# The channel mixer's residual of layer 1, prepared per token tile beside feature tiles 4 to 7

## The chip, the cores and the metric

One NeuronCore of a Trainium2 chip runs the whole program. The time is that of one execution on the device in microseconds (us). TensorE (PE, with its weight loads as PEld), VectorE (DVE), ScalarE (ACT) and GpSimd (POOL) each work through a queue of their own in order and wait for each other by semaphores; SyncE (SP) issues nearly all DMAs, also in order.

## The reference

A decoder trunk of two layers over 1024 tokens of width 1024. Layer 1 (`l == 0` in the code) has an RWKV-7 mixer, layer 2 (`l == 1`) a sparse attention; each is followed by a dense channel mixer. What matters here:

```
x   = layernorm(ALPHA * x + (1 + gt1) * mixer(hin), ln_g[i, 0], ln_b[i, 0])
hin = x * (1 + sc2) + sh2
y   = (silu(hin @ w_gate) * (hin @ w_up)) @ w_out          # 1024 -> 2816 -> 1024
x   = layernorm(ALPHA * x + (1 + gt2) * y, ln_g[i, 1], ln_b[i, 1])
```

shift, scale and gate come from a projection of the conditioning vector by `ada_w`, whose parts for later sub-layers the kernel computes while the channel mixer of layer 1 runs.

## The kernel before

Everything is float32. A matrix product is made of three passes: each operand is split into a rounded part `hi` and a rest `lo`, and hi*hi, hi*lo and lo*hi are added in PSUM. For weights, ACT casts a loaded tile (`wst`, 3 buffers) to `whi`, and `wlo` is the difference, formed on DVE twice and on POOL once in every three (list `low`).

The channel mixer is `ffn`. Tokens go in two halves (`hf`) of 512, each four token tiles of 128. The 2816 hidden features are 22 feature tiles of 128, in three groups (`FG`: 0 to 7, 8 to 14, 15 to 21). For each feature tile `j` of a group `gate_up` makes 24 + 24 matmuls into the two banks `psu`: the gate, which ACT evacuates by silu, and the up product, which DVE multiplies onto it (tile `sl`, L1167) and splits into `hid`. The gate of tile j+1 may overwrite the gate's bank as soon as silu is done; the up product of tile j+1 needs the other bank, and so L1167 of tile j. After a group, the hidden tiles are multiplied by rows of `w_out` (banks `psg` and `psx`), and `evac_y` adds the result times the gate vector `G` onto the residual tiles `R`.

The residual (`resid`, L799 and L800) takes the normalised, not yet scaled rows of the sub-layer before and applies gain and bias in place: two POOL operations on 128x1024 for each token tile. `ln_tiles` loads the gate vector `G` (from DRAM, where `ada_done` put it), and the gain and bias rows of the layer norm, spread over 128 partitions, into two tiles of the pool `z4` (8 buffers of 128x1024, function `big`), and multiplies both by ALPHA on DVE (L783, L784). In the first half the rows are there already (`zt`, tiles `R` that the input preparation also reads); in the second each is loaded from DRAM (L798) into a buffer `R` (4) once the first half has written its own.

In the text, all of this stands once per half behind the loop over feature tiles 0 to 7. In the same loop stand pieces of the `ada_w` projection (`ada_v`, L300 to L311): four loads of 128x1024 into `z4` tiles and eight DVE operations on 128x512 (L305, L307) each. They stand at feature tiles 4, 6 and every second one from 8 in the first half, and at 0, 2, 4, 6, 8 in the second. The pool `z4` opens only when the tail of the RWKV mixer is through, beside feature tile 3 of the first half.

A planner sets the order on each engine: it walks through a modelled time and gives an engine, whenever it is free, the instruction that stands first in the text among those whose operands and buffers are ready. So an instruction can be placed well before others that stand ahead of it in the text. The order is fixed then; on the chip an engine waits at an instruction until its semaphores say it can start.

Of the kernel before, what the change touches and what calls it, by code (L numbers as in the profile page):

```python
# [24 lines left out]
NTT = HN // P  # L25
# [51 lines left out]
def dap(ap, off, dims):  # L77
    return bass.AP(tensor=ap.tensor, offset=ap.offset + off, ap=[list(d) for d in dims])
# [3 lines left out]
def trunk(ctx, tc, a, out):  # L82
# [3 lines left out]
    def pool(st, name, bufs=1, space=None, side=None):  # L86
        kw = {} if space is None else {"space": space}
        if side:
            kw["side"] = side
        return st.enter_context(tc.tile_pool(name=name, bufs=bufs, reuse_waits="tile", **kw))  # L90
# [23 lines left out]
    def act(o, i, f=AF.Identity, **kw):  # L114
        return A.activation(o, i, f, **kw)  # L115
# [8 lines left out]
    def hilo(hi, lo, x, eng=G):  # L124
        V.tensor_scalar(hi, x, 1.0, None, op0=OP.mult)
        sub(eng, lo, x, hi)
# [112 lines left out]
    def proj_fm(w, off, ld, xhi, xlo, ncol=P, c=slice(0, 512)):  # L239

        wh, wl = wcols(w, off, ld, ncol)
        o = psx(bank[0])
        for k in range(KT):
            mm3(o[:ncol, c], wh[k], wl[k], xhi[k][:, c], xlo[k][:, c], k == 0, k == KT - 1)
        return o
# [525 lines left out]


    gbp = pool(ctx, "gb", side="right")
    def ln_tiles(l, s, big):
        g = gbp.tile([P, D], F32, tag="G", name="G")
        dma(g, dap(modd[l], (24 * s + 16) * P, [[0, P], [1, D]]))
        if 2 * l + s == 0:
            return g, None, None
        i = 2 * l + s - 1
        lg, lb = big(), big()  # L780
        dma(lg, dap(a["ln_g"], i * D, [[0, P], [1, D]]))
        dma(lb, dap(a["ln_b"], i * D, [[0, P], [1, D]]))
        V.tensor_scalar(lg, lg, ALPHA, None, op0=OP.mult)  # L783
        V.tensor_scalar(lb, lb, ALPHA, None, op0=OP.mult)  # L784
        return g, lg, lb

    def resid(l, s, hf, tt, lnt, r=None):

        held = r is not None
        if not held:  # L790
            r = p2.tile([P, D], F32, tag="R", bufs=2, name="R") if l + s == 0 else rtile()
        i = 2 * l + s
        if i == 0:
            dma(r, a["x"][0, hf * HN + tt * P:hf * HN + tt * P + P, :])
            V.tensor_scalar(r, r, ALPHA, None, op0=OP.mult)
        else:
            if not held:
                dma(r, zd[i - 1][hf][tt * P:tt * P + P, :])  # L798
            G.tensor_tensor(r, r, lnt[1], op=OP.mult)  # L799
            G.tensor_tensor(r, r, lnt[2], op=OP.add)  # L800
        return r
# [57 lines left out]
    def big():  # L859
        return bp[0].tile([P, D], F32, tag="z4", bufs=8, name="z4")  # L860
# [3 lines left out]
    def rtile():  # L864
        return rz.tile([P, D], F32, tag="R", bufs=4, name="R")
# [41 lines left out]
    if True:  # L907
# [181 lines left out]
        lnt = {}  # L1089
# [14 lines left out]
        for gc in range(17):  # L1104
            hf, c = gc // 8, gc % 8
# [13 lines left out]
            if gc == 14:  # L1119
                zt = [rtile() for _ in range(NTT)]  # L1120
# [34 lines left out]
    def ffn(l, hfs, zt, step=lambda gate: None, x=None, pairs=False):  # L1155
        with ExitStack() as st:
            tp = pool(st, f"ffn{l}{hfs[0]}")
            yt = lambda: tp.tile([P, 512], F32, tag="yt", bufs=2, name="yt")
            win, wo = a["ffn_w_in"], a["ffn_w_out"]
            bi, bo_ = l * D * 2 * FH, l * FH * D  # L1160

            def gate_up(j, c, h_, l_):
                og = proj_fm(win, bi + j * P, 2 * FH, *x, c=c)
                sl = tp.tile([P, HN], F32, tag="sl", bufs=2, name="sl")
                act(sl[:, c], og[:, c], AF.Silu)
                ou = proj_fm(win, bi + FH + j * P, 2 * FH, *x, c=c)
                V.tensor_tensor(sl[:, c], sl[:, c], ou[:, c], op=OP.mult)  # L1167
                hilo(h_[:, c], l_[:, c], sl[:, c], V)

            for hf in hfs:  # L1170
                for g, (j0, j1) in enumerate(FG):
                    hh, hl = [], []
                    hid = lambda: tp.tile([P, HN], F32R, tag="hid", bufs=16, name="hid")
                    if g == 0 and pairs:
                        for q in range(2):
                            if q:
                                hin_pair(2 * l + 1, q, zt, *x)
                            for j in range(NPAIR):
                                if q == 0:
                                    hh.append(hid())  # L1180
                                    hl.append(hid())
                                gate_up(j, slice(q * 256, q * 256 + 256), hh[j], hl[j])
                                step(hl[j])
                    after = lastg[0]
                    for j in range(j0 + len(hh), j1):
                        hh.append(hid())
                        hl.append(hid())
                        gate_up(j, slice(0, HN), hh[-1], hl[-1])
                        step(hl[-1])
                        if l == 0 and hf == 0 and j in (4, 6):  # L1190
                            ada_v(0, 8 + j // 2, big, yt)
                            if j == 6:
                                ada_done(0, yt, 40, 48)
                        if l == 0 and hf == 0 and j >= 8 and j % 2 == 0:
                            ada_v(1, j // 2 - 4, big, yt)
                        if l == 0 and hf == 1 and j < 10 and j % 2 == 0:
                            ada_v(1, 7 + j // 2, big, yt)
                        if l == 0 and hf == 1 and j == 10:
                            ada_done(1, yt)
                            hin_vec(1, 0)  # L1200
                            hin_vec(1, 1)
                            bt.append(bias_table(hf32))
                        if l == 0 and hf == 1 and j >= 10:
                            take(bt[0], 1)
                    if g == 0:
                        lnt = ln_tiles(l, 1, big)
                        with tc.issue_after(after.ins) if pairs else ExitStack():
                            rr = [resid(l, 1, hf, tt, lnt, zt[tt] if hf == hfs[0] else None) for tt in range(NTT)]
                    if g == 2 and hf != hfs[-1]:
                        x = hin_prep(2 * l + 1, hf + 1)  # L1210
                    for tt2, n in ([(None, 0), (None, 1)] if g < 2 or l == 0 else [(0, 0), (0, 1), (1, 0), (1, 1)]):
                        tts = range(NTT) if tt2 is None else range(2 * tt2, 2 * tt2 + 2)
                        o = quad() if tt2 is None else [psg(), psx("gx"[n])]
                        for k2 in range(0, j1 - j0, 2):
                            nk = min(2, j1 - j0 - k2)
                            wh, wl = wrows(wo, j0 + k2, nk, bo_ + n * 512, D)
                            step(wl[0])
                            for i_, tt in enumerate(tts):
                                for i in range(nk):
                                    k = k2 + i  # L1220
                                    mm3(o[i_], hh[k][:, tt * P:tt * P + P], hl[k][:, tt * P:tt * P + P],
                                        wh[i], wl[i], k == 0, k == j1 - j0 - 1)
                        for i_, tt in enumerate(tts):
                            evac_y(rr[tt], o[i_], n, lnt, yt)
                        if tt2 is not None and n == 1:
                            if l == 1 and tt2 == 0:
                                fin.clear()
                                for nm in ("ln_g", "ln_b"):
                                    fin.append(big())
                                    dma(fin[-1], dap(a[nm], 3 * D, [[0, P], [1, D]]))  # L1230
                            for tt in tts:
                                if l == 1 and hf == 0 and tt2 == 1:
                                    pend.append((l, 1, hf, tt, rr[tt]))
                                else:
                                    layernorm(l, 1, hf, tt, rr[tt], tp)
                if l == 0:
                    for tt in range(NTT):
                        layernorm(l, 1, hf, tt, rr[tt], tp)
# [9 lines left out]
    with kw:  # L1248
# [346 lines left out]
        zt, x = attention(0)  # L1595
# [4 lines left out]
        zt, x = attention(1)  # L1600
# [28 lines left out]
```

## Time and profile before

| | us |
|---|---|
| median of 3 runs | 3300.29 (3296.58 to 3302.11) |
| the profiled execution | 3298.0 |
| its span from first to last instruction | 3296.2 |
| PE busy | 3057.3 (93%) |
| DVE busy | 2171.1 (66%) |
| POOL busy | 993.3 (30%) |
| channel mixer of layer 1 | about 990 to 1800 of the span |

Times in the rows below count from the start of the span. Busy time on PE is that of pipelined matmuls: two that follow each other at full rate start 0.23 us apart although each lasts 0.39 us.

### The profile page before, as it was taken

Reading aid. Unit: us, or ns where it says so; the run is one execution under the profiler, and the core shown is the slowest. Engines: PE = TensorE matmul, PEld = TensorE weight load, DVE = VectorE, ACT = ScalarE, POOL = GpSimd, SP = SyncE. Lnnn points to the kernel's source line nnn. Section 1 sums busy time; section 2 is a strip of 40 time slices with the busy share of each in tenths; the row PEclk is TensorE's granted clock in tenths of the full one; section 3 lists DMA queues with packets and bytes.
Section 4 is the critical chain, followed back from the end, with each engine's and each line's share of the span. In section 5 each row is a group of like instructions: output and inputs, shape, how many; then the busy total and the mean of one; then the engine's idle time right before and its main releaser. Section 6 shows DMA issues by size and latency. Waiting matters only on the chain. (4 is left out here: it accounts for less than half of the span.)

```text
span 3296.2 us, 48948 instructions
## 1 busy us (share of the span) xinstructions
PE 3057.3 (93%) x17857; PEld 2416.9 (73%) x17857; DVE 2171.1 (66%) x4255; ACT 1350.1 (41%) x2510; POOL 993.3 (30%) x780
## 2 busy tenths in 40 slices
PE   7887999889999999999899999988999999899998
PEld 2465467677877788888688776677887777687886
DVE  4676988647776765494245487886697788775345
ACT  3552463234444222332223655647522566452223
POOL 3351254101113411241113213555222432443111
PEclk8988989979999999999999999998999999999999
DMA  6465465788864665382534432154333421253333
GB/s 196 135 190 152 105 193 142 150 157 178 177 153 121 214 198 161 117 272 90 122 97 127 144 90 68 60 156 122 97 95 105 138 63 34 92 168 100 93 99 122
DMA packets 603460, 436.33 MB, mean 132 GB/s; under 512 B 200338, under 2 KB 500882, under 8 KB 603218
## 3 DMA queue, kind: packets, MB, share of 16 engines
q1 hardware_dynamic: 603218, 433.19, 46.7%
q8 instruction: 141, 2.31, 0.3%
q14 instruction: 101, 0.83, 0.1%
HBM read 378.07 MB, written 54.90 MB: 131 GB/s over the span
## 5 line engine op out<-in xcount | busy, mean ns | idle before, releaser
L204 ACT CAST whi<-wst 128x512 fp32r<-128x512 f32 x886 | 540.5, 619 | 1229.8 <-PE psu L234 533.5
L121 POOL TENSOR_TENSOR wlo<-wst,whi 128x512 fp32r<-128x512 f32 x330 | 459.0, 1391 | 1514.6 <-ACT whi L204 1472.7
L121 DVE TENSOR_TENSOR wlo<-wst,whi 128x512 fp32r<-128x512 f32 (+1 forms) x556 | 474.4, 857 | 509.1 <-ACT whi L204 504.0
L233 PE MATMUL psu<-hin,whi 128*128 128x512 f32 (+1 forms) x1568 | 584.7, 373 | 45.6 <-DVE sl L1167 29.2
L234 PE MATMUL psu<-hin,whi 128*128 128x512 f32 (+1 forms) x1568 | 584.4, 373 | 9.8 <-DVE hin L900 3.3
L235 PE MATMUL psu<-hin,wlo 128*128 128x512 f32 (+1 forms) x1568 | 582.2, 371 | 0.1
L233 PEld LDWEIGHTS psu<-hin,whi 128*128 128x128 f32 x1568 | 299.5, 191 | 101.1 <-DVE sl L1167 32.6
L234 PEld LDWEIGHTS psu<-hin,whi 128*128 128x128 f32 x1568 | 300.2, 191 | 60.6 <-DVE hin L900 3.5
L235 PEld LDWEIGHTS psu<-hin,wlo 128*128 128x128 f32 x1568 | 300.3, 192 | 50.4 <-POOL wlo L121 0.6
L234 PE MATMUL psg<-wlo,hid 128*128 128x512 f32 x528 | 206.3, 391 | 0.0
L233 PE MATMUL psg<-whi,hid 128*128 128x512 f32 x528 | 205.1, 391 | 0.0
L235 PE MATMUL psg<-whi,hid 128*128 128x512 f32 x528 | 205.0, 389 | 0.0
L233 PE MATMUL psg<-xs,whi 128*128 128x512 f32 x384 | 163.2, 434 | 19.4 <-ACT whi L204 10.7
L234 PE MATMUL psg<-xs,whi 128*128 128x512 f32 x384 | 162.9, 425 | 13.2 <-POOL xs L121 10.6
L235 PE MATMUL psg<-xs,wlo 128*128 128x512 f32 x384 | 161.9, 422 | 3.0 <-DVE wlo L121 3.0
L1167 DVE TENSOR_TENSOR sl<-sl,psu 128x512 f32<-128x512 f32 (+1 forms) x98 | 61.7, 630 | 140.2 <-PE psu L235 131.0
L233 PEld LDWEIGHTS psg<-xs,whi 128*128 128x128 f32 x384 | 77.0, 201 | 53.4 <-ACT whi L204 13.5
L233 PEld LDWEIGHTS psg<-whi,hid 128*128 128x128 f32 x528 | 99.1, 188 | 21.0
L235 PEld LDWEIGHTS psg<-whi,hid 128*128 128x128 f32 x528 | 99.1, 188 | 20.8
L234 PEld LDWEIGHTS psg<-wlo,hid 128*128 128x128 f32 x528 | 99.2, 188 | 20.6 <-DVE wlo L121 0.4
L115 ACT ACTIVATE z<-z,mx 128x128 f32<-128x128 f32 (+7 forms) x128 | 99.2, 776 | 33.0 <-DVE mx L1532 32.0
L234 PEld LDWEIGHTS psg<-xs,whi 128*128 128x128 f32 x384 | 76.9, 200 | 42.2 <-POOL xs L121 14.5
(417 smaller groups left out, 6500.7 us busy)
## 6 DMA issues: line engine op xcount, KB each, us to landing
wst<-in_ffn_w_in_dram SPq DMA_DIRECT2D x196, 512.0 KB
wst<-in_ffn_w_out_dram SPq DMA_DIRECT2D x92, 512.0 KB
z<-in_ada_w_dram SPq DMA_DIRECT2D x56, 512.0 KB
wst<-in_rwkv_w_rkv_dram SPq DMA_DIRECT2D x48, 512.0 KB
wst<-in_rwkv_w_out_dram SPq DMA_DIRECT2D x64, 256.0 KB
wst<-in_dsa_w_out_dram SPq DMA_DIRECT2D x32, 512.0 KB
wst<-in_dsa_w_in_dram SPq DMA_DIRECT2D x26, 512.0 KB
wst<-in_ada_w_dram SPq DMA_DIRECT2D x24, 512.0 KB
```

The lines of the kernel that those rows point to most:

```text
L115: return A.activation(o, i, f, **kw)
L121: i = eng.tensor_tensor(lo, x, hi.bitcast(F32), op=OP.subtract)
L204: A.copy(h_[:, :m], st[:, c:c + m])
L233: mm(o, lh, rh, start=first, stop=False)
L234: mm(o, lh, rl, start=False, stop=False)
L235: mm(o, ll, rh, start=False, stop=last)
L1167: V.tensor_tensor(sl[:, c], sl[:, c], ou[:, c], op=OP.mult)
```

## The change

`ln_tiles` is cut in two: the part that loads and scales gain and bias becomes `ln_aff`, and `ln_tiles` takes its result when there is one. In layer 1, in both halves, `ln_aff` now stands in the loop right behind feature tile 4, ahead of that tile's `ada_v`; and `resid` of token tile 0 to 3 stands behind feature tile 4, 5, 6 and 7. The gate vector `G` is loaded where it was. Layer 2 keeps its order.

```diff
-    def ln_tiles(l, s, big):
+    def ln_tiles(l, s, big, aff=None):
         g = gbp.tile([P, D], F32, tag="G", name="G")
         dma(g, dap(modd[l], (24 * s + 16) * P, [[0, P], [1, D]]))
         if 2 * l + s == 0:
             return g, None, None
+        return (g,) + (aff or ln_aff(l, s, big))
+
+    def ln_aff(l, s, big):
         i = 2 * l + s - 1
         lg, lb = big(), big()
         dma(lg, dap(a["ln_g"], i * D, [[0, P], [1, D]]))
         dma(lb, dap(a["ln_b"], i * D, [[0, P], [1, D]]))
         V.tensor_scalar(lg, lg, ALPHA, None, op0=OP.mult)
         V.tensor_scalar(lb, lb, ALPHA, None, op0=OP.mult)
-        return g, lg, lb
+        return lg, lb
...
                     after = lastg[0]
+                    if g == 0:
+                        rr = []
                     for j in range(j0 + len(hh), j1):
                         hh.append(hid())
                         hl.append(hid())
                         gate_up(j, slice(0, HN), hh[-1], hl[-1])
                         step(hl[-1])
+                        if l == 0 and g == 0 and j >= 4:
+                            if j == 4:
+                                aff = ln_aff(l, 1, big)
+                            rr.append(resid(l, 1, hf, j - 4, (None,) + aff, zt[j - 4] if hf == hfs[0] else None))
                         if l == 0 and hf == 0 and j in (4, 6):
                             ada_v(0, 8 + j // 2, big, yt)
...
                     if g == 0:
-                        lnt = ln_tiles(l, 1, big)
+                        lnt = ln_tiles(l, 1, big, aff if rr else None)
                         with tc.issue_after(after.ins) if pairs else ExitStack():
-                            rr = [resid(l, 1, hf, tt, lnt, zt[tt] if hf == hfs[0] else None) for tt in range(NTT)]
+                            rr = rr or [resid(l, 1, hf, tt, lnt, zt[tt] if hf == hfs[0] else None) for tt in range(NTT)]
```

## Rows read from the trace of the kernel before

**Rows 1.** The page, part 1: busy us (share of the span) xinstructions.
```profile
PE 3057.3 (93%) x17857; PEld 2416.9 (73%) x17857; DVE 2171.1 (66%) x4255; ACT 1350.1 (41%) x2510; POOL 993.3 (30%) x780
```

**Rows 2.** Windows: length, busy us (x) of PE, PEld, DVE, ACT, POOL; clock, DMA.
```profile
1076.35:1091.73 15.38, 15.38 (x74) 12.82 (x73) 14.99 (x22) 4.10 (x7) 2.58 (x3) 1.00 1.06 366
1091.73:1115.40 23.67, 19.19 (x82) 15.47 (x81) 23.60 (x12) 4.22 (x7) 23.67 (x10) 0.93 0.58 191
...
1120.00:1200.00 80.00, 80.00 (x358) 66.36 (x358) 49.15 (x70) 19.55 (x32) 12.70 (x9) 1.00 0.61 189
...
1400.00:1440.00 40.00, 40.00 (x186) 33.36 (x184) 36.21 (x66) 15.25 (x22) 10.84 (x9) 1.00 0.81 270
1440.00:1480.00 40.00, 39.34 (x178) 32.30 (x178) 39.67 (x38) 9.27 (x16) 29.53 (x13) 1.00 0.86 279
```

**Rows 3.** Timeline of PE around its stall: start, length, instruction [idle before <- releaser].
```profile
1099.19 0.39 PE L235 MATMUL psu<-hin,wlo 128*128 128x512 f32 x1
1104.06 0.66 PE L233 MATMUL psu<-hin,whi 128*128 128x512 f32 x1 [4.48 <-DVE sl L1167]
...
1107.80 0.39 PE L233 MATMUL psu<-hin,whi 128*128 128x512 f32 x1
```

**Rows 4.** Timeline of POOL in the first half.
```profile
1085.58 1.29 POOL L121 TENSOR_TENSOR wlo<-wst,whi 128x512 fp32r<-128x512 f32 x1 [6.80 <-ACT whi L204]
1091.73 11.13 POOL L799 TENSOR_TENSOR R<-R,z 128x1024 f32<-128x1024 f32 x4 [4.86 <-DVE z L783]
1102.82 2.80 POOL L800 TENSOR_TENSOR R<-R,z 128x1024 f32<-128x1024 f32 x1
1105.58 1.46 POOL L121 TENSOR_TENSOR wlo<-wst,whi 128x512 fp32r<-128x512 f32 x1
1107.00 8.43 POOL L800 TENSOR_TENSOR R<-R,z 128x1024 f32<-128x1024 f32 x3
```

**Rows 5.** Timeline of DVE in the same stretch.
```profile
1076.35 0.49 DVE L305 TENSOR_SCALAR yt<-z,csr 128x512 f32<-128x512 f32 x1 [1.00 <-DMA z<-in_ada_w_dram]
1076.87 4.82 DVE L307 SCALAR_TENSOR_TENSOR yt<-z,csr,yt 128x512 f32<-128x512 f32 x5
...
1083.65 0.68 DVE L1167 TENSOR_TENSOR sl<-sl,psu 128x512 f32<-128x512 f32 x1
...
1090.96 0.69 DVE L783 TENSOR_SCALAR z<-z 128x1024 f32<-128x1024 f32 x1
...
1092.16 2.89 DVE L307 SCALAR_TENSOR_TENSOR yt<-z,csr,yt 128x512 f32<-128x512 f32 x1
1094.98 2.89 DVE L784 TENSOR_SCALAR z<-z 128x1024 f32<-128x1024 f32 x1
...
1100.58 2.82 DVE L121 TENSOR_TENSOR wlo<-wst,whi 128x512 fp32r<-128x512 f32 x1
1103.33 0.67 DVE L1167 TENSOR_TENSOR sl<-sl,psu 128x512 f32<-128x512 f32 x1
```

**Rows 6.** Timeline of SP's issues in the first half.
```profile
1070.07 5.25 SPq L300 DMA_DIRECT2D z<-in_ada_w_dram  x4
...
1075.88 3.70 SPq L300 DMA_DIRECT2D z<-in_ada_w_dram  x4
1079.67 0.65 SPq L781 DMA_DIRECT2D z<-in_ln_g_dram  x1
```

**Rows 7.** Timeline of SP's issues in the second half.
```profile
1416.83 1.10 SPq L300 DMA_DIRECT2D z<-in_ada_w_dram  x2
...
1429.08 0.53 SPq L798 DMA_DIRECT2D R<-z  x1
...
1440.21 3.26 SPq L781 DMA_DIRECT2D z<-in_ln_g_dram  x1
...
1444.00 0.90 SPq L798 DMA_DIRECT2D R<-z  x2
```

**Rows 8.** Timeline of PE at its stall in the second half.
```profile
1457.32 0.50 PE L233 MATMUL psu<-hin,whi 128*128 128x512 f32 x1 [0.66 <-DVE sl L1167]
```

## The prediction

> **What bounds the kernel now.** The first view to read is the busy time of the engines. PE is busy for 93% of the span and DVE for 66% [rows 1]: what makes the kernel longer or shorter is what makes PE wait. The second is a table of windows through the channel mixer of layer 1. Where only weights and hidden tiles are worked on, PE has no idle time and runs at full clock (80.00 of 80.00 us in 1120 to 1200). In the two stretches with the residual it loses time: 19.19 busy of 23.67 us at a granted clock of 0.93 in the first half, 39.34 of 40.00 in the second. In both DVE is busy throughout (23.60 of 23.67 and 39.67 of 40.00) [rows 2].
>
> The third view is the timeline of each engine through 1076 to 1115. PE stops at 1099.4 and starts again at 1104.06, an idle time of 4.48 us that the multiplication L1167 on DVE ends [rows 3]. L1167 is what hands the up product's bank back. The up product of feature tile 5 was through some 10 us earlier: PE had meanwhile done the 24 matmuls of the next gate, 24 x 0.227 = 5.45 us. These 5.45 us are the slack that DVE has at each L1167. Why was DVE late? Its queue ahead of L1167 holds two pieces of the `ada_w` projection, 16 operations, all of which run between 1076.35 and the L1167 of 1103.33. From 1091.73 on, its operations on SBUF take 2.8 to 2.9 us in place of 0.69: L783 and L784 are the same operation on the same shape, and one takes 0.69, the other 2.89 us [rows 5]. 1091.73 is the moment at which POOL starts the eight operations of the residual (11.13 + 2.80 + 8.43 us, with one `wlo` of 1.46 between) [rows 4]. In these 23.67 us DVE gets 12 instructions done, and in the 15.38 us ahead of them 22 [rows 2]. L1167, which reads PSUM, still takes 0.67 us [rows 5]. So while POOL works on SBUF, DVE gets about one SBUF operation through for each of POOL's, and a DVE operation costs 2.87 - 0.69 = 2.2 us more.
>
> After the stall, nine matmuls take from 1104.06 to 1107.80, 3.74 us against 9 x 0.227 = 2.04 at full rate [rows 3]: 1.7 us at the lower of the two clock levels, after an engine idle for 4.5 us. The second half loses 0.66 us [rows 8], with no visible slow matmuls.
>
> So the block costs 4.5 + 1.7 + 0.7 = 6.9 us today. That is all that the best outcome could return.
>
> **The change part by part.** No instruction is added or taken away: two loads, two DVE operations and eight POOL operations per half, and four row loads in the second half, change place only. What counts is where the planner puts them. It does not follow the text: the residual stands behind feature tile 7, yet POOL begins it at 1091.73 [rows 4], while PE is in the up product of tile 5 (L1167 at 1083.65 is that of tile 4, the one at 1103.33 that of tile 5 [rows 5]). It ran two feature tiles early because POOL is mostly idle and the operands were there. What held it back were the gain and bias rows: L781 is issued at 1079.67, behind eight loads of `ada_w` that fill the eight buffers of `z4` [rows 6]. In the text the change puts these two loads ahead of those eight, but the four token tiles still have the same operands, and all are ready together. So I expect no spreading: I expect the same block of about 23 us, earlier.
>
> First half, when: the loads go out at 1070.07, where the first `ada_w` load goes now, in place of 1079.67. That first load was used by DVE at 1076.35, which waited for it [rows 5, 6]; the gain lands at about the same time, L783 follows at 1076 to 1077, and POOL starts near 1077, 15 us earlier, to end near 1101.
>
> First half, price: the whole block then lies ahead of the L1167 of 1103.33. In 23.7 us go 23.7/2.87 = 8 slow DVE operations; four of these are paid ahead of that L1167 already (1092.16, 1094.98, one more L307 and 1100.58 [rows 5]). Four more, at 2.2 us, make 8.8 us. DVE has no idle time to absorb them (14.99 busy of 15.38 us [rows 2]), the slack of 5.45 us is used up already, and there is nothing later to give the time back, since behind this L1167 PE did not wait again. Against it: two of the eight `ada_w` tiles find their buffer held by gain and bias, and their four operations (4 x 0.75 = 3 us) may slip behind that L1167. Bounds: 0 - 6.2 us if the block were hidden completely, and + 8.8. I take 8.8 less a quarter of the 3 us, + 8.0.
>
> Second half: L781 goes from 1440.21 to the place of the `ada_w` load at 1416.83 [rows 7]. The rows of the first two token tiles can come in at about 1430, as now (the second is issued at 1429.08); those of the last two are loaded at 1444.00 [rows 7], since their buffers wait for the first half's results. So four POOL operations move ahead, from behind 1450 to about 1430 to 1441, and the other four stay near their place. Ahead of the L1167 that PE waits for at 1457.32 [rows 8], DVE has three slow operations now and would have about six: 3 x 2.2 = 6.6 us. But DVE is not full in the stretch ahead (36.21 of 40.00 us in 1400 to 1440 [rows 2]), so part is absorbed. Bounds - 0.7 and + 6.6; I take the middle, + 3.0.
>
> Nothing else moves by more than that. The gate vector's load stays behind `ada_done`. POOL's `wlo` can queue behind up to two residual operations (5.6 us), but it did so before (1105.58 behind five [rows 4]). SP's order is changed by two loads of 0.65 us or less of issue.
>
> By the Trainium skill (SBUF — State Buffer, section "SBUF: two separate sides") the port pair that DVE and GpSimd share is an exclusive lock: whoever starts first keeps it for the whole instruction and the other blocks. The trace agrees, 2.89 against 0.69 us. By that rule alone the eight operations cost DVE some 8 x 2.2 = 17.6 us per half wherever they stand, so moving them sheds nothing by itself and the sum hangs only on the slack at their new place.
>
> **Sum.** 3298.0 (the profiled execution, its span of 3296.2 and 1.8 around it) + 8.0 + 3.0 = 3309.0. The median of the runs shown is 2.3 us above the profiled one; on that scale 3311.3.
>
> **The rivals.**
>
> *It spreads, and is faster.* If the planner keeps POOL's operations two by two beside feature tiles 4 to 7, each tile brings DVE two slow operations, 4.4 us, inside the slack of 5.45. Then both stalls and the slow matmuls go: 3300.3 - 6.9 = 3293.4. For it: the text asks for that order, and POOL's own `wlo` stand between. Against it: the residual ran two tiles ahead of its place in the text. It decides from the point where fewer than three slow operations fall between two L1167.
>
> *It moves and costs the same.* If the slow operations are `ada_w` pieces that the order, with gain and bias loaded first, leaves behind the next L1167, DVE's lateness there stays what it is: 3300.3, give or take 3. For it: the loads of `ada_w` come up to two issues later. Against it: DVE has no reserve from 1076 to 1103.
>
> *The weights run late too.* SP issues in order. If slow `ada_w` operations hold their `z4` buffers, the next `ada_w` load waits at the head of SP's queue, and the weight loads stand behind it. One feature tile's loss is 10.9 us (48 x 0.227): 3311.3 + 10.9 = 3322. For it: the DMA engines are already full there (share 1.06 [rows 2]). Against it: the weights have three buffers.
>
> **How the numbers follow.** The block moves and costs more: 0.50, with its own range 3304 to 3318 (the halves' bounds, without the ends of both). Spread: 0.17. Same: 0.25. Weights late: 0.08. The time is that of the first, 3311. From 3292 to 3322 the range takes in the spread case at its lower end, the late weights at its upper end, and leaves out under 2 in 10. A change of under 0.2% (6.6 us) can't be told from none by these measurements. Faster by more: 0.17 (the spread case). Within it: 0.25 and 0.05 of the first case, in all 0.30. Slower: 0.45 + 0.08 = 0.53.
>
> **What would show it.** In the first half, gain and bias issued near 1070, and POOL's eight operations in one run from near 1077; DVE's L307 at 2.8 us from there on; a wait of PE for L1167's successor of 8 to 14 us, followed by slow matmuls. In the second half, gain and bias near 1417, POOL's run torn in two, and a wait of 2 to 7 us. Wrong would be: two POOL operations beside each of four feature tiles with PE unbroken (the spread case); the same block with PE's wait at 4 to 5 us (the same case); or a wait of PE that ends with a weight load's cast in place of L1167 (late weights).

## The result and the profile after

The changed kernel takes 3322.32 us (median of 6 runs, 3320.25 to 3327.29) against 3298.08 for the kernel before on the same chip (6 runs, 3290.0 to 3302.11): a ratio of 1.0076, 95% interval 1.0065 to 1.0088. It is slower, as forecast, but by some 25 us where 11 were forecast, and just outside the range, which ended at 3322. The profiled execution has a span of 3321.3 us, 25.1 more than before. No engine has more to do: DVE was busy for 2171.1 us and is now for 2167.1, and POOL has lost 0.8 us [rows 1].

First the page, part 1, of the kernel after, and its windows over two stretches (length, busy us and count of PE, PEld, DVE, ACT, POOL, then the granted clock, DMA share and GB/s):

```profile
PE 3060.8 (92%) x17857; PEld 2419.9 (73%) x17857; DVE 2167.1 (65%) x4255; ACT 1350.9 (41%) x2510; POOL 992.5 (30%) x780
```

```profile
1050.00:1140.00 90.00, 79.33 (x334) 64.76 (x333) 59.59 (x72) 23.71 (x38) 36.11 (x20) 0.91 0.64 211
1400.00:1500.00 100.00, 89.82 (x383) 73.81 (x382) 78.23 (x107) 25.96 (x40) 41.28 (x23) 0.91 0.74 242
```

PE stands still for more than 10 us in each of the two stretches, and the clock falls to 0.91 in both. (Lines of `kernel.py` from the cut on are 3 higher: L1170 was L1167, L802 and L803 were L799 and L800, L786 and L787 the scaling of gain and bias.)

SP in the first half. Gain and bias go out at 1070.68, first of all, where they went at 1079.67 behind eight loads of `ada_w` [rows 6]:

```profile
1070.68 0.42 SPq L784 DMA_DIRECT2D z<-in_ln_g_dram  x1
1071.15 1.33 SPq L785 DMA_DIRECT2D z<-in_ln_b_dram  x1
1074.97 1.92 SPq L300 DMA_DIRECT2D z<-in_ada_w_dram  x4
```

POOL in the first half. Nothing has spread: the same block in one run, from 1077.25 to 1102.2, 14.5 us earlier than [rows 4]:

```profile
1077.25 10.55 POOL L802 TENSOR_TENSOR R<-R,z 128x1024 f32<-128x1024 f32 x4 [4.95 <-DVE z L786]
1087.76 1.71 POOL L121 TENSOR_TENSOR wlo<-wst,whi 128x512 fp32r<-128x512 f32 x1
1089.44 8.30 POOL L803 TENSOR_TENSOR R<-R,z 128x1024 f32<-128x1024 f32 x3
...
1099.39 2.83 POOL L803 TENSOR_TENSOR R<-R,z 128x1024 f32<-128x1024 f32 x1
```

DVE in the same stretch. From L305 on each operation on SBUF waits its turn; two L307 take 5.58 us where five took 4.82 [rows 5]. The L1170 of feature tile 4 starts at 1095.44, in place of 1083.65:

```profile
1080.47 2.27 DVE L305 TENSOR_SCALAR yt<-z,csr 128x512 f32<-128x512 f32 x1 [0.27 <-DMA z<-in_ada_w_dram]
1082.77 5.58 DVE L307 SCALAR_TENSOR_TENSOR yt<-z,csr,yt 128x512 f32<-128x512 f32 x2
1088.27 1.75 DVE L121 TENSOR_TENSOR wlo<-wst,whi 128x512 fp32r<-128x512 f32 x1
1089.95 5.57 DVE L307 SCALAR_TENSOR_TENSOR yt<-z,csr,yt 128x512 f32<-128x512 f32 x2
1095.44 0.68 DVE L1170 TENSOR_TENSOR sl<-sl,psu 128x512 f32<-128x512 f32 x1
```

PE in the first half, around its two waits, in place of the one of 4.48 us [rows 3]. The second is for the last operation of an `ada_w` piece, whose sum over partitions PE forms (L310). After each wait a run of eleven 128x512 matmuls starts 0.43 us apart, not 0.23, at a granted clock of 0.50 (windows 1096.17 to 1100.60 and 1106.27 to 1110.68):

```profile
1096.17 0.79 PE L233 MATMUL psu<-hin,whi 128*128 128x512 f32 x1 [7.81 <-DVE sl L1170]
1096.76 0.63 PE L234 MATMUL psu<-hin,whi 128*128 128x512 f32 x1
...
1100.60 0.43 PE L234 MATMUL psu<-hin,whi 128*128 128x512 f32 x1
1104.57 1.84 PE L310 MATMUL pst<-ones,yt 128*128 128x1 f32 x8 [2.86 <-DVE yt L307]
1106.27 0.77 PE L235 MATMUL psu<-hin,wlo 128*128 128x512 f32 x1
...
1110.68 0.50 PE L233 MATMUL psu<-hin,whi 128*128 128x512 f32 x1
```

The second half starts 10.5 us late (its first L307 at 1425.48, in place of 1415.02). POOL's block is torn by the arrival of the rows, and its eight operations lie between 1443.7 and 1475.9:

```profile
1443.69 2.39 POOL L802 TENSOR_TENSOR R<-R,z 128x1024 f32<-128x1024 f32 x1 [5.72 <-DMA R<-z]
...
1453.47 2.46 POOL L803 TENSOR_TENSOR R<-R,z 128x1024 f32<-128x1024 f32 x1
...
1459.23 2.59 POOL L802 TENSOR_TENSOR R<-R,z 128x1024 f32<-128x1024 f32 x1 [1.63 <-DMA R<-z]
...
1473.21 2.68 POOL L803 TENSOR_TENSOR R<-R,z 128x1024 f32<-128x1024 f32 x1
```

The third and the fourth L1167 of this half in the kernel before; the fourth is the one that PE waited for [rows 8]:

```profile
1439.61 0.68 DVE L1167 TENSOR_TENSOR sl<-sl,psu 128x512 f32<-128x512 f32 x1
1456.59 0.68 DVE L1167 TENSOR_TENSOR sl<-sl,psu 128x512 f32<-128x512 f32 x1
```

After the change the third comes at 1459.52 and the fourth at 1479.60. Behind the third, DVE still has most of the last `ada_w` piece to do, and it has no idle time to catch up in: the last line is its window (fourth number: 38.63 busy of 38.81 us).

```profile
1459.52 0.68 DVE L1170 TENSOR_TENSOR sl<-sl,psu 128x512 f32<-128x512 f32 x1
...
1463.35 0.47 DVE L305 TENSOR_SCALAR yt<-z,csr 128x512 f32<-128x512 f32 x1
...
1466.28 4.59 DVE L307 SCALAR_TENSOR_TENSOR yt<-z,csr,yt 128x512 f32<-128x512 f32 x2
1470.80 2.88 DVE L121 TENSOR_TENSOR wlo<-wst,whi 128x512 fp32r<-128x512 f32 x1
1473.60 6.08 DVE L307 SCALAR_TENSOR_TENSOR yt<-z,csr,yt 128x512 f32<-128x512 f32 x4
1479.60 0.68 DVE L1170 TENSOR_TENSOR sl<-sl,psu 128x512 f32<-128x512 f32 x1
...
1441.47:1480.28 38.81, 28.68 (x123) 23.34 (x121) 38.63 (x33) 8.01 (x14) 27.81 (x12) 0.86 0.82 271
```

PE waits twice, 4.02 us for the third and 6.17 us for the fourth, where it waited 0.66 us for the fourth alone [rows 8], and each time 13 or 14 matmuls follow at the slower pace:

```profile
1460.25 0.80 PE L233 MATMUL psu<-hin,whi 128*128 128x512 f32 x1 [4.02 <-DVE sl L1170]
...
1465.54 0.56 PE L233 MATMUL psu<-hin,whi 128*128 128x512 f32 x1
...
1480.34 0.79 PE L233 MATMUL psu<-hin,whi 128*128 128x512 f32 x1 [6.17 <-DVE sl L1170]
...
1486.05 0.55 PE L234 MATMUL psu<-hin,whi 128*128 128x512 f32 x1
```

Where the 25.1 us are, from these rows. A stretch of n slow intervals is priced at its length less n x 0.227 us:

| | before | after | difference |
|---|---|---|---|
| first half, PE's waits | 4.5 | 7.8 + 2.9 | + 6.2 |
| first half, slow matmuls | 1.7 | 4.43 - 2.27 and 4.41 - 2.27 | + 2.6 |
| second half, PE's waits | 0.7 | 4.0 + 6.2 | + 9.5 |
| second half, slow matmuls | 0 | 5.29 - 2.72 and 5.71 - 2.95 | + 5.3 |
| sum | 6.9 | 30.5 | + 23.6 |

Of the rest of 1.5 us, 0.6 lie ahead of the change (the L1167 of feature tile 3 starts at 1071.53 before and at 1072.15 after). The other 0.9 are the eight small matmuls L310 behind the second wait of the first half, at a granted clock of 0.50 too: from the first of them to the next large matmul 1.70 us go by, and in the kernel before 0.81:

```profile
1086.68 0.94 PE L310 MATMUL pst<-ones,yt 128*128 128x1 f32 x8
1087.49 0.49 PE L235 MATMUL psu<-hin,wlo 128*128 128x512 f32 x1
```

### The profile page after: what moved, and what is told of

Same layout as the page of the kernel before. It is cut to its first block, busy times and chain, and to the rows that moved or that the text cites. A ratio compares the mean times of both kernels' runs of the same rounds, so it can differ in the third digit from the quotient of the medians.

```text
span 3321.3 us, 48951 instructions
## 1 busy us (share of the span) xinstructions
PE 3060.8 (92%) x17857; PEld 2419.9 (73%) x17857; DVE 2167.1 (65%) x4255; ACT 1350.9 (41%) x2510; POOL 992.5 (30%) x780
## 5 line engine op out<-in xcount | busy, mean ns | idle before, releaser
L121 DVE TENSOR_TENSOR wlo<-wst,whi 128x512 fp32r<-128x512 f32 (+1 forms) x556 | 467.3, 844 | 518.7 <-ACT whi L204 510.0
L1170 DVE TENSOR_TENSOR sl<-sl,psu 128x512 f32<-128x512 f32 (+1 forms) x98 | 61.8, 630 | 152.3 <-PE psu L235 143.1
```

The source lines that it names most:

```text
L121: i = eng.tensor_tensor(lo, x, hi.bitcast(F32), op=OP.subtract)
```

## The experiments

All are compared with runs of the kernel before on the same chip; the ratio is what counts, since the medians of the kernel before are some 4 us higher on these chips than the 3298 of the expectations (3301.63, 3302.11 and 3302.73 us in the three groups).

**Which part of the change moves the block?** e1 moves the loads and the scaling of gain and bias alone:

```diff
-                        if l == 0 and g == 0 and j >= 4:
-                            if j == 4:
-                                aff = ln_aff(l, 1, big)
-                            rr.append(resid(l, 1, hf, j - 4, ...))
+                        if l == 0 and g == 0 and j == 4:
+                            aff = ln_aff(l, 1, big)
...
-                        lnt = ln_tiles(l, 1, big, aff if rr else None)
+                        lnt = ln_tiles(l, 1, big, aff if l == 0 else None)
```

> Only the loads and scaling of gain and bias go to feature tile 4, ahead of that tile's ada_w piece; the residual stays in one block behind the loop, as in the kernel before. Theory (the place of the two loads sets the place of POOL's block, and the block's coincidence with the ada_w pieces on DVE is what costs): as the changed kernel, 3322 give or take 4, with POOL's first residual operation near 1077. Rival (it is the residual's own new place in the text that costs): as before, 3298 give or take 4.

Measured: 3326.8 us against 3301.63, ratio 1.0077 (1.0063 to 1.0091), the changed kernel's loss. With the residual's lines back behind the loop, POOL's block begins 2.4 us behind that of the changed kernel, still 12 us ahead of that of the kernel before (timeline of POOL, e1):

```profile
1079.63 10.52 POOL L802 TENSOR_TENSOR R<-R,z 128x1024 f32<-128x1024 f32 x4 [6.54 <-DVE z L786]
```

So the early loads are enough for the whole loss, and the new place of the residual in the text adds nothing that can be measured.

e2 leaves the residual in the loop, but puts it and the loads behind the `ada_w` piece of tile 6:

```diff
-                        if l == 0 and g == 0 and j >= 4: ...
...
                             ada_v(1, 7 + j // 2, big, yt)
+                        if l == 0 and g == 0 and j >= 6:
+                            if j == 6:
+                                aff = ln_aff(l, 1, big)
+                            for tt in ((0, 1, 2) if j == 6 else (3,)):
+                                rr.append(resid(l, 1, hf, tt, ...))
```

> Gain, bias and the residual of token tiles 0 to 2 stand at feature tile 6, that of tile 3 at tile 7, all behind the ada_w piece of tile 6: still in the loop, per tile, but the z4 buffers go to the ada_w pieces first. Theory: the block starts about where it started before (near 1091 in the first half), so 3298 give or take 4. Rival (standing in the loop, ahead of the later weights' lo parts on POOL, is what costs): most of the 24 us remains, 3312 or more.

Measured: 3301.37 us, ratio 1.0000 (0.9991 to 1.0010). The block begins at 1094.23 (timeline of POOL, e2):

```profile
1094.23 11.12 POOL L802 TENSOR_TENSOR R<-R,z 128x1024 f32<-128x1024 f32 x4 [4.85 <-DVE z L786]
```

**The halves.** e3 and e4 make the change in one half of the tokens:

```diff
-                        if l == 0 and g == 0 and j >= 4:
+                        if l == 0 and hf == 0 and g == 0 and j >= 4:     # e3; hf == 1 in e4
```

> The change in the first half of the tokens alone. Theory: the two halves cost what their stretches of the two traces show, about 10 us here: 3308 give or take 3. Rival (the damage runs through what the first half hands on to the second, its R tiles and z4 buffers): over 15 us here, or nearly none.

> The change in the second half alone. Theory: about 15 us, 3313 give or take 3, with two waits of PE for DVE of about 4 and 6 us, each followed by some 13 matmuls at the lower clock level. Rival (the second half suffers only because the first runs late): under 8 us.

Measured: e3 1.0027 (1.0017 to 1.0038), some 9 us; e4 1.0053 (1.0039 to 1.0066), some 17 us (by the medians 7.5 and 15.2). They add up to the whole (0.27% + 0.53% against 0.76%), so the second half doesn't suffer from the first. In e4 PE waits for DVE as in the changed kernel's second half, beside the 4.5 us that the unchanged first half keeps: 7.2 us in two waits for L1170 and 2.7 for a piece's last L307, 9.9 in all, where two waits of 4 and 6 were expected.

**Contention, or buffers held for long?** In e5 and e6 the residual of this stage is done by DVE itself, at the changed kernel's place and at the old one:

```diff
-            G.tensor_tensor(r, r, lnt[1], op=OP.mult)
-            G.tensor_tensor(r, r, lnt[2], op=OP.add)
+            e_ = V if (l, s) == (0, 1) else G
+            e_.tensor_tensor(r, r, lnt[1], op=OP.mult)
+            e_.tensor_tensor(r, r, lnt[2], op=OP.add)
```

> The changed kernel with the residual's eight operations per half of layer 1's channel mixer on DVE in place of POOL. Loads, buffers and SP's order stay early; what goes is POOL's work on SBUF beside DVE, and DVE gets 8 x 1.22 = 9.8 us of its own in place of 8 x 2.2 = 17.6 us of lateness per half. Theory (contention of POOL and DVE): it gets back a good third to half of the 24 us, 3308 to 3314. Rival (the two z4 buffers held for long make the ada_w and weight loads late): no gain, 3320 or more.

> The kernel before with the residual's operations of layer 1's channel mixer on DVE. Theory: the block's 17.6 us of lateness on DVE become 9.8, so part of the 6.9 us that it cost goes: 3292 to 3298. Rival: DVE, busy through the whole stretch, is the bound there, and work put on it adds: 3302 or more.

Measured: e5 0.9979 (0.9970 to 0.9988), e6 0.9978 (0.9969 to 0.9987). Without POOL's residual beside DVE the early place costs nothing that can be measured, and both beat the kernel before by some 7 us, e6 as expected. I had expected e5 to recover a half at most: that was far too little. The windows of e5 show why. PE has lost 1.15 of 90 us, and DVE, which does eight more operations, is busy for 59.24 us, no longer than the 59.59 of the changed kernel:

```profile
1050.00:1140.00 90.00, 88.85 (x396) 72.57 (x396) 59.24 (x87) 26.40 (x42) 19.64 (x13) 1.00 0.69 225
```

e7 keeps the block on POOL and on the old loads, but holds it behind POOL's last `lo` part of feature tiles 0 to 7; e9 does the same with the early loads of e1:

```diff
-                        with tc.issue_after(after.ins) if pairs else ExitStack():
+                        with tc.issue_after(after.ins if pairs else lastg[0].ins):
```

> The kernel before, with POOL's residual block of layer 1 held until POOL's last lo part of feature tiles 0 to 7 is through, so that it runs beside the first matmuls of the output product, behind the ada_w pieces of tiles 4 and 6. Theory: the waits of 4.5 and 0.7 us and the slow matmuls go, since DVE has room there: 3291 give or take 3. Rival (the output product then waits for the lo parts behind the block, or evac_y for R): 3298 or more.

> Gain and bias are loaded and scaled at feature tile 4 as in the changed kernel, but POOL's residual block is held behind the last lo part of feature tiles 0 to 7. The two z4 buffers are thus held even longer, and SP's order is that of the early loads; only POOL's block is away from the ada_w pieces. Theory (contention at the block's place is all of it): as with the block held alone, 3291 give or take 4. Rival (a good part of the second half's loss is the two held buffers, which bring the ada_w tiles and the weights late): 3303 or more.

Measured: e7 3291.25 us, 0.9965 (0.9951 to 0.9979), the fastest with nothing left out: some 11 us under the kernel before, where its waits and slow matmuls come to 6.9, which the interval just reaches. e9 0.9972 (0.9960 to 0.9983), not to be told from e7. So the early loads and the two `z4` buffers that they hold are harmless by themselves; they harm because they let the block begin early. In e7 the block begins at 1098.41, 6.7 us after that of the kernel before (4.5 us counted from the L1167 of feature tile 4, which starts at 1085.82 in e7), with the last L307 of the pieces done, and PE does not wait at all in either stretch (windows of e7):

```profile
1050.00:1140.00 90.00, 90.00 (x406) 74.41 (x405) 67.18 (x80) 26.40 (x42) 40.74 (x22) 1.00 0.69 229
1400.00:1500.00 100.00, 100.00 (x458) 83.24 (x457) 83.60 (x115) 29.87 (x47) 43.06 (x24) 1.00 0.71 228
```

e12 combines the hold with e6's edit, the residual on DVE:

```diff
-                        with tc.issue_after(after.ins) if pairs else ExitStack():
+                        with tc.issue_after(after.ins if pairs else lastv[0].ins):
```

> The kernel before with layer 1's channel mixer residual on DVE and held behind DVE's last operation of feature tiles 0 to 7. Theory: PE waits for DVE in neither half, as with the block held on POOL, so nothing is left to gain: 3291 give or take 3. Rival (the block on POOL still slows DVE and POOL's lo parts unseen): 3287 or less.

Measured: 0.9967 (0.9952 to 0.9982), the same as e7. Once PE doesn't wait, it doesn't matter who does the residual.

**The pieces themselves.** e10 and e11 are the changed kernel and the kernel before without seven of the `ada_w` pieces:

```diff
-                            ada_v(0, 8 + j // 2, big, yt)
+                            V.memset(modf[:, 0, 32 + 2 * j:36 + 2 * j], 0.0)
...
-                            ada_v(1, 7 + j // 2, big, yt)
+                            V.memset(modf[:, 1, 28 + 2 * j:32 + 2 * j], 0.0)
```

> The changed kernel with the ada_w pieces at feature tiles 4 and 6 of the first half and 0 to 8 of the second left out, loads and DVE operations both; a memset stands for their result, so the kernel leaves out that part of the computation. Theory (the block costs by falling among these pieces): with DVE free of them the early block costs next to nothing, and this run and the next differ by less than 4 us, both some 5 to 10 us below 3298. Rival (the early block costs by itself, as POOL's lo parts queue behind it): 15 us or more above the next.

> The kernel before without the same pieces. Theory: within 4 us of the run before it. Rival: 15 us or more below it.

Measured: 3285.5 and 3285.07 us, ratios 0.9945 (0.9933 to 0.9956) and 0.9942 (0.9928 to 0.9955). The 24 us between the two kernels are gone although the early block is still there, in one run from 1081.00 to 1105.9 (timeline of POOL, e10):

```profile
1081.00 10.84 POOL L802 TENSOR_TENSOR R<-R,z 128x1024 f32<-128x1024 f32 x4 [6.00 <-DVE z L786]
```

PE's only wait in e10's two stretches ends with a `lo` part on POOL; that is the rival's mechanism, at 0.77 us (timeline of PE, e10):

```profile
1103.16 0.50 PE L235 MATMUL psu<-hin,wlo 128*128 128x512 f32 x1 [0.77 <-POOL wlo L121]
```

Both are some 18 us under the kernel before, more than the 5 to 10 expected. Of e11's, 6.9 are the waits and slow matmuls. Some 6 more are work on PE that goes with the pieces: e11 has 56 L310 matmuls fewer, eight for each piece, and eight of them take 0.81 us of PE's time (1086.68 to 1087.49 above). The other 5 stay open.

**Would real spreading have helped?** e8 ties each token tile's residual on POOL behind the last `lo` part of its feature tile:

```diff
+                            with tc.issue_after(lastg[0].ins):
+                                rr.append(resid(l, 1, hf, j - 4, (None,) + aff, ...))
```

> The changed kernel with each token tile's residual tied on POOL behind the last lo part of its feature tile: now the spreading that the text asks for really happens. Theory (the same eight slow operations fall among the same ada_w pieces, only thinner): DVE has no idle time there, so most of the loss stays, 3308 to 3320. Rival (4.4 us per feature tile lie inside the 5.45 us of slack): 3293 give or take 4.

Measured: 1.0018 (1.0006 to 1.0030), some 6 us: neither what the theory expected (10 us or more) nor the rival. The halves part ways. In the first, PE still waits (timeline of PE, then of POOL, e8):

```profile
1099.84 0.79 PE L233 MATMUL psu<-hin,whi 128*128 128x512 f32 x1 [7.70 <-DVE sl L1170]
...
1115.26 0.50 PE L233 MATMUL psu<-hin,whi 128*128 128x512 f32 x1 [0.88 <-DVE sl L1170]
```

```profile
1082.03 2.40 POOL L802 TENSOR_TENSOR R<-R,z 128x1024 f32<-128x1024 f32 x1 [5.95 <-DVE z L786]
...
1086.09 2.58 POOL L802 TENSOR_TENSOR R<-R,z 128x1024 f32<-128x1024 f32 x1
1088.61 5.61 POOL L803 TENSOR_TENSOR R<-R,z 128x1024 f32<-128x1024 f32 x2
...
1095.85 2.79 POOL L802 TENSOR_TENSOR R<-R,z 128x1024 f32<-128x1024 f32 x1
```

The tie did not make pairs here. Between the L1170 of feature tile 3 (1075.93) and that of tile 4 (1099.11), the one that PE waits for, POOL does five residual operations.

In the second it doesn't wait at all: the pairs begin at 1450.85, 1468.07, 1477.50 and 1485.50, one behind each of the L1170 at 1449.13, 1465.63, 1475.12 and 1484.20, and no L1170 comes more than the slack late (windows of e8):

```profile
1400.00:1500.00 100.00, 100.00 (x457) 83.18 (x457) 85.16 (x116) 30.21 (x47) 44.10 (x25) 1.00 0.79 255
```

So where two POOL operations fall between two L1170, as the rival asks, PE does not wait. But only the first pair falls among operations of the pieces, whose last L307 ends at 1468.7: what pairs would cost beside a full DVE queue in all four places isn't shown.

## Why the prediction was right in its way and wrong in its size

- *What bounds the stage; what a POOL operation costs DVE.* Right. e5 and e6 take away POOL's share and the cost is gone, e10 and e11 take away the pieces and the difference is gone. L307, which reads two tiles in SBUF, takes up to 2.9 us beside POOL, and L1170, which reads one in SBUF and one in PSUM, 0.68. By the Trainium skill (SBUF — State Buffer, section "SBUF: two separate sides") the port pair of DVE and GpSimd is a lock held for a whole instruction, which DVE's operations take if they have two SBUF inputs or run in a 2-port performance mode. The trace agrees, with 2.9 us for L307 and 0.68 for L1170.
- *The block moves and does not spread.* Right: forecast near 1077, found at 1077.25. e1 shows the cause, the place of the two loads, and e2, with the loads late, that a place inside the loop costs nothing by itself.
- *First half, + 8.0.* + 8.8 in the table, 9.7 with the slow L310, and some 9 in e3. That the size is right is in part luck. The waits grew by 6.2 us, and the rest are matmuls at the lower clock level, which the forecast had not added. And the long wait lies one feature tile ahead of the forecast's: it is for the L1170 of tile 4 (1095.44), while that of tile 5, the successor of the 1103.33 that was priced, comes at 1111.32 and holds up nothing.
- *Second half, + 3.0 with a bound of + 6.6.* This is the step that failed: + 14.9 in the traces, some 17 in e4. Three things in it. I let half of the cost of four early operations be absorbed, but DVE had no idle time there (38.63 busy of 38.81 us). I counted lateness up to one L1167, the fourth of the half, which PE waits for today. PE already waited at the third: the first four POOL operations came ahead of it, as forecast, it starts 9.4 us late (19.9 less the 10.5 by which the half starts late), and 4.0 of these became a wait of PE. The other four, which I had left near their place, came early too and fell among the rest of the pieces, and PE waited 6.2 us more at the fourth. And the slow matmuls behind both waits, 5.3 us, were not in the sum.

  Late loads are not behind it. The next loads of `ada_w` do go out late, but DVE waits for none: the first operation of the last piece, L305 at 1463.35 (1441.76 before), comes late because it stands a few instructions behind the late third L1170 in DVE's queue. Nor is it the two buffers that gain and bias hold: in e9, with the same early loads and the block held, this L305 starts at 1440.26, in a half that starts 2.6 us earlier than before (its first L307 at 1412.46 against 1415.02), so some 1 us late.
- *The clock.* The slow matmuls of the old wait stood in the forecast as a gain (1.7 us); those of the new waits were left out. They are 4.3 + 5.3 us, 8 more than before and a third of the loss, without the 0.9 of L310.
- *The best outcome.* 6.9 us were called all that could come back. e7, with no wait left, returns some 11; its interval just reaches 6.9, so whether there is more stays open.
- *The rivals.* Spreading did not happen. When it was forced (e8), pairs came about in the second half only, and there PE did not wait. "Moves and costs the same" is refuted by the result and by e1. Late weights: PE's waits in these stretches ended with L1170 or L307, none with the cast of a weight tile, and e9, with the same early loads, is not slow. That the range came within 0.3 us of the time is luck: its end of 3322 is the price of this case, which did not happen. The case that did happen was given an end of 3318, and the bounds of its two halves alone make 3300.3 + 8.8 + 6.6 = 3315.7.

## What to carry to other kernels

When an instruction is hoisted by a planner, its place in the text says little: look for what it waits for (here a buffer and a load) and ask where it lands once that comes earlier. In this case each POOL operation on SBUF held up about one DVE operation (2.8 us in place of 0.7), and that was free only where DVE's queue had room ahead of the next instruction that PE needs; count the lateness up to every such instruction in the stretch, not up to the first. And price a wait of PE with the slow matmuls behind it.

## What the runs showed of the hardware that was not expected

- After waits of 2.9 to 7.8 us in the kernels before and after, PE ran 9 to 14 matmuls of 128x512 at the lower of its two clock levels (starts 0.43 us apart); after waits of 0.66 us in the kernel before and 0.88 in e8 none. The five long waits of the kernels before and after make 25.3 us, and the slow matmuls behind them another 11.3. In e4 a wait of 1.95 us was enough too: five matmuls start at the full clock, and eight follow at the lower one (granted clock 0.51 from 1456.94 to 1460.33).
- The residual is dearer to DVE when POOL does it than when DVE does it itself: in 1050 to 1140 DVE is busy for 62.67 us in the kernel before (first line) and for 59.70 in e6 (second line), with eight operations of 128x1024 more.

```profile
1050.00:1140.00 90.00, 85.52 (x377) 70.20 (x376) 62.67 (x74) 25.40 (x41) 38.63 (x21) 0.98 0.67 222
1050.00:1140.00 90.00, 89.67 (x402) 73.83 (x401) 59.70 (x87) 26.40 (x42) 21.54 (x14) 1.00 0.68 227
```
